# The low part of a weight block: a subtraction on GpSimd, or ScalarE's negative and an adding DMA

## The chip, the core and the metric

The kernel runs on one core of a Trainium2 chip. The metric is device time in microseconds (us) of one execution. The core has a matrix engine (TensorE, rows PE and, for its weight loads, PEld), VectorE (DVE), ScalarE (ACT), GpSimd (POOL) and a queue engine (SP). Each engine works through its own instructions in the order written and waits on semaphores for the others. Copies between memories are done by 16 DMA engines; an instruction on SP, ACT or POOL issues such a copy.

## The reference, cut to what matters

The reference is a two-layer trunk over 1024 tokens of width 1024. What bears on the change is the feed-forward block with a gated unit that ends each layer (width 2816), run twice:

```python
def conv_ffn(h, w_up, conv_w, conv_b, w_down):
    a = dwconv3(h @ w_up, conv_w, conv_b)
    g, u = jnp.split(a, 2, axis=-1)
    return (jax.nn.silu(g) * u) @ w_down
```

The output projection of layer 0's mixer and layer 1's spatial-gating mixer also hold products `h @ W` that are made in the same way.

## The kernel before, in words

**Precision.** TensorE multiplies numbers of a shortened float type (`F32R`, fp32r in the rows). To keep the accuracy of full floats, every operand x is split in two: the high part is x rounded to fp32r, the low part is x minus the high part. A product is then three matmuls into one accumulator, high by high, high by low and low by high (`mm3`). The split is made by `hilo` (line 1149): ScalarE writes the high part into the first half of a new buffer (`A.copy`, line 1152), and VectorE or GpSimd subtracts it from x into the second half (the helper at line 128 issues every plain subtraction, addition and product). The engine that subtracts is chosen by strings of V and G near the top of the file.

**Products.** From the output projection of layer 0 on, every product with a weight takes seven products of half-sized blocks, M1 to M7, in the order M1, M2, M6, M7, M4, M5, M3 (a Strassen scheme). M1 and M2 use blocks of W as they are loaded. Before M6, `wsums` (line 1280) forms S3, S2, S1 and S4 on VectorE, and writes S3, S1 and S4 over the blocks they come from: S3 over the block that M1's split read, S4 over the one that M2's split read. A sum can so start only once the split of that block has read it.

**Up phases** (`up_steps`, line 1289). An up phase of a feed-forward block goes through 22 pairs of 128-wide column tiles of `w_up`; a pair is 7 steps, one per product, of 12 matmuls each, 84 in all. `prep` splits the step's block of W. `use` does the matmuls and then adds the result into the pair's tiles on VectorE (ScalarE for M1). After M3 the pair goes to `post`: for the two tiles a convolution over time (one ScalarE operation, line 1520, and two VectorE operations, line 124, each), Silu on ScalarE (line 1532), a product of the two tiles on VectorE, and, for every second pair, `spill` (line 1410): sums on GpSimd and stores to DRAM that ScalarE issues.

**Down phases** (`down_steps`, line 1344) work through k for each product; a step is again 12 matmuls. Here the other operand is split as well, on GpSimd where it comes from the spilled blocks.

**Who subtracts.** `E_W` gives for each up phase one letter per product M1 to M7, `E_D` for each down phase one letter for k modulo 4:

```python
E_W, E_D = ("VGGVGGG", "VGGVGGG", "GGGVGGG"), ("GVGV", "VVGV", "GVGV", "GVGV", "GVGV")
```

So GpSimd makes 5 of 7 low parts of W in a pair of the first feed-forward block and 6 of 7 in the second one, where M1 is among them.

**Order.** `run` (line 1180) walks through the steps: loads run 8 or 9 steps ahead in the up phases, `prep` 3 steps ahead with a raised priority, and pieces of earlier pairs' convolutions are put in between (`Later`). A scheduler turns this into one fixed order per engine; buffers (`unit`, 40 of 512 KB) are reused as they come free.

Of the kernel before, what the change touches and what calls it, by code (L numbers as in the profile page):

```python
# [20 lines left out]
P = 128  # L21
# [15 lines left out]
# for each phase: how many steps its loads run ahead, and what is made of them, for each product  # L37
# [16 lines left out]
# which of VectorE and GpSimd takes a piece of work: a string for each of the norms, of the phases  # L54
# [15 lines left out]
# Packed per-feature vectors: name, number of 128-row columns.  # L70
# [18 lines left out]
def tile_kernel(ctx: ExitStack, tc: tile.TileContext, ap: dict, out: bass.AP, stop=None):  # L89
# [32 lines left out]
    # ------------------------------------------------------------------ helpers  # L122
# [33 lines left out]
    def eager(main, side):  # L156
        """Emit side as early as its inputs allow (it yields True while they don't)."""
        live = True
        while live:
            for blocked in side:  # L160
                if blocked:
                    break
            else:
                side = iter(())
            try:
                next(main)
            except StopIteration:
                live = False
        for _ in side:
            pass  # L170
# [20 lines left out]
    def mtile(ps, w, hhi, hlo, n=S):  # L191
        """ps [P, n] = W[:, m-tile]^T h, from the unit w of [P, (k, 128)]."""
# [6 lines left out]
    # modulation vectors: 48 columns a layer, and 16 for the context's first norm  # L199
# [25 lines left out]
    def rstd_bcast(acc, n, scale, tp, newps, dg):  # L225
        """acc [P, n], sums of squares -> PSUM [P, n], rstd in every row. dg: [P, n] of scratch."""
# [12 lines left out]
    def bcast(R, r, nt, dg):  # L239
        """R [P, nt*128]: in every row the values of r [P, nt], one column after the other."""  # L240
# [7 lines left out]
    # ================================================================ layer 0  # L248
# [4 lines left out]
    # the blocks of C a product belongs to: (i, l), or (i,) for both l  # L253
# [3 lines left out]
    Hd = dram.tile([2, 2, 2, P, 2048], F32, name="Hd")          # order, half, parity of m  # L257
# [3 lines left out]
    Qd = dram.tile([HEADS, 2, P, S], F32, name="Qd")            # head, hi | lo  # L261
# [9 lines left out]
    def gated_sum(x, gate):  # L271
        """accum for x += gate * C"""
# [10 lines left out]
    def layer0_front(fp):  # L283
        with ExitStack() as es:
# [27 lines left out]
            # ---- filter's network; x^T, context, first modulation columns (shift and scale), norms  # L312
# [4 lines left out]
            def filter_mlp():  # L317
                """sin(f (x w + b)) twice, both halves of time side by side; -> h2s: hi above lo."""
# [10 lines left out]
                def layer(l, rhs, w):  # L329
# [5 lines left out]
                    # u: the angle in turns; less its nearest integer  # L335
# [82 lines left out]
            # ---- DFT over 8 residues of time: frequencies (k + 1/2) pi/1024 + m pi/4, k < 128.  # L418
            # Complex values are R - iS; parts of a tile [P, R|S, 4, CH].
# [6 lines left out]
            def dft(z, n):  # L426
                """z [P s, 8 r, CH] -> X for m = 0, 2, 4, 6 and for m = 1, 7, 5, 3."""
# [37 lines left out]
            def dft_part(z, w, n):  # L465
                """R (w = 0) or S (w = 1) alone -> [P, (m even | m odd), 4, CH]."""
# [14 lines left out]
                add(e(), t[:, 0, 0:2], a[:, w, 0:2], a[:, w, 2:4])      # c0 c1  # L481
                sub(e(), t[:, 0, 2], a[:, w, 0], a[:, w, 2])            # d0
                sub(e(), t[:, 0, 3], a[:, x, 1], a[:, x, 3])            # d1, the other part
# [5 lines left out]
                pm(e(), t[:, 1, 0], b[:, w, 0], b[:, x, 2])             # e0  # L489
                mp(e(), t[:, 1, 1], b[:, w, 0], b[:, x, 2])             # e1  # L490
                u = a
                sub(e(), u[:, 0, 0], b[:, w, 1], b[:, w, 3])            # p
                add(e(), u[:, 0, 1], b[:, x, 1], b[:, x, 3])            # q, the other part
                pm(e(), u[:, 1, 0], u[:, 0, 0], u[:, 0, 1])             # u
                mp(e(), u[:, 1, 1], u[:, 0, 0], u[:, 0, 1])             # v
# [4 lines left out]
            def filters():  # L500
                h2r = h2s.rearrange("p (s r) -> p r s", r=8)
                for o in range(2):
# [14 lines left out]
                    for half in range(2):  # L517
# [4 lines left out]
                        for sd in range(2):  # L522
# [8 lines left out]
                            if sd == 0:  # L531
                                # time 0 has the forward tap alone, (s + d) / 2, and the skip
# [15 lines left out]
            # ---- Hyena's chain: spectrum, product, inverse, gate  # L548
            zs, done = {}, set()

            def spectrum(X, o, half, n):
                """Y = X H, in place."""
# [14 lines left out]
            def idft(Y, n):  # L567
                """Y (m = 0, 2, 4, 6; m = 1, 7, 5, 3) -> Q for r < 4 and for r >= 4."""
# [3 lines left out]
                add(e(), t[:, :, 0:2], ye[:, :, 0:2], ye[:, :, 2:4])   # f0 g0  # L572
                sub(e(), t[:, :, 2:4], ye[:, :, 0:2], ye[:, :, 2:4])   # f1 g1
# [9 lines left out]
                add(e(), u[:, :, 0:2], yo[:, :, 0:2], yo[:, :, 2:4])   # f0 g0  # L583
                sub(e(), u[:, :, 2:4], yo[:, :, 0:2], yo[:, :, 2:4])   # f1 -g1
                O = yo
                add(e(), O[:, :, 0], u[:, :, 0], u[:, :, 1])           # D0
                sub(e(), O[:, :, 2], u[:, :, 0], u[:, :, 1])           # D2
                d = f8()
                sub(e(), d[:, 0, 0], u[:, 0, 2], u[:, 1, 3])           # D1
                add(e(), d[:, 1, 0], u[:, 1, 2], u[:, 0, 3])  # L590
                add(e(), d[:, 0, 1], u[:, 0, 2], u[:, 1, 3])           # D3
                sub(e(), d[:, 1, 1], u[:, 1, 2], u[:, 0, 3])
                add(e(), O[:, 0, 1], d[:, 0, 0], d[:, 1, 0])           # sqrt(2) O1
                sub(e(), O[:, 1, 1], d[:, 1, 0], d[:, 0, 0])
                sub(e(), O[:, 0, 3], d[:, 1, 1], d[:, 0, 1])           # sqrt(2) O3
# [52 lines left out]
            # lambda = exp(q1.k1) - exp(q2.k2) + lambda_init, negated, in every row  # L648
# [11 lines left out]
            # ---- the input projection  # L660
# [11 lines left out]
            def to_time(a):  # L672
                """[P ch, t] -> PSUM [P s, 8 r, P ch], t = 8 s + r."""
# [119 lines left out]
    def attention(fp, x):  # L793
        """x: gets the stream's tiles, to which the first two products of the output projection are added."""
        with ExitStack() as es:
# [39 lines left out]
            def load_head(h):  # L835
                """K: (hi, hi) and (lo, lo), Q: (hi, lo), one above the other, for either map; V."""
# [18 lines left out]
            # A tile of 128 queries goes through: scores and their softmax's sums (m = 0, 1); the maps' difference,  # L855
            # a tile later; its transposes, LAG tiles later; and four tiles together through the values.
# [14 lines left out]
            def factors(q):  # L871
                """p0 - lambda l0/l1 p1, still to be divided by l0"""
# [25 lines left out]
            def values(q):  # L898
                """Six pieces, three a tile, for the two tiles that q ends."""
# [8 lines left out]
            def headnorm(g):  # L908
                """The head's norm, and its way out, in pieces."""
# [17 lines left out]
            # M1, M2 and M6 of the output projection, and what they need  # L927
            wb, spare, aux = {}, [], None

            def two_rows(src, k, n=2):  # L930
                """Tiles k and k + 1 of src's rows."""
# [13 lines left out]
            def operand(name, src):  # L945
                """Loads four tiles of rows; then their parts, one a piece."""
# [11 lines left out]
            def operand3(name, a, b, c, op, tag, last=None):  # L958
                """Of a + b - c (op: add) or a - b + c, likewise; last: tile 3 of a where it isn't in DRAM."""
# [26 lines left out]
            def product(m):  # L986
                """Four pieces of 12 matmuls."""
# [139 lines left out]
    # ================================================================ the rest  # L1127
    # Products W^T h take seven products of half-sized blocks (Strassen's scheme in Winograd's form):
# [31 lines left out]
    class Later:  # L1160
# [3 lines left out]
        @classmethod  # L1164
        def add(cls, gen, wait=0):
            cls.gens.append([gen, wait])
# [258 lines left out]
    def in_place(s, m, k, y, z, t3, first="M6"):  # L1425
# [9 lines left out]
        elif m == "M4":  # L1435
            sub(E(E_J[s], k), z[:, H0], z[:, H0], y[:, H0])    # T4
# [353 lines left out]
```

## Time and profile before

| | |
|---|---|
| median of 3 runs | 2897.93 us (2897.4 to 2901.98) |
| the profiled execution, first to last instruction | 2897.8 us |
| PE busy | 2461.0 us, 85% |
| DVE busy | 2345.8 us, 81% |
| ACT busy | 1075.4 us, 37% |
| POOL busy | 1624.7 us, 56% |
| moved by DMA | 363.93 MB |

The span of the profiled execution and the median of the runs agree to 0.2 us, so nothing that matters lies around the span. Busy time is the time in which an engine had an instruction at work; PE's matmuls overlap, so the mean duration of one is longer than its share of the busy time. An idle time in a row is put down to what ended it: "idle 21.8 <-POOL u L128" is time in which the engine waited for a GpSimd instruction of line 128 that wrote a buffer u.

### The profile page before, as it was taken

To read this page: it belongs to the slowest core of one execution; us is meant where nothing else is said; L and a number is where in the kernel's file an instruction comes from. 1 tells how busy PE (TensorE), PEld (TensorE's weight loads), DVE (VectorE), ACT (ScalarE), POOL (GpSimd) and SP (SyncE) were. 2 spreads that over 40 slices of the span, in tenths; PEclk is the share of its full clock that TensorE was granted. 3 is DMA by queue.
4 is the path that set the end of the run, shared out by engine and by line. 5 is a ranking of instruction groups with operands and counts; after the bars stand their busy time and mean duration, and the time that the engine had idled before them with its cause. 6 is when DMAs were issued, how large, how long until landed. Compare 5 with 4: busy or idle time off the path is not lost. (4 is left out here: it accounts for less than half of the span.)

```text
span 2897.8 us, 29893 instructions
## 1 busy us (share of the span) xinstructions
PE 2461.0 (85%) x10776; PEld 1949.6 (67%) x10776; DVE 2345.8 (81%) x2467; ACT 1075.4 (37%) x1561; POOL 1624.7 (56%) x986
## 2 busy tenths in 40 slices
PE   6899667777988679999998799899669999999897
PEld 2897556565766457777776687677547777776676
DVE  4666887866998889999998987859988888887944
ACT  2322011015764344433343344532254343344242
POOL 1323565545444755645556787535665655657785
PEclk9899878888999889999999999999889999999999
DMA  7243121256732412434347654153021323227322
GB/s 269 69 143 114 66 87 46 84 183 200 209 122 84 174 65 78 161 122 149 118 145 255 231 164 129 44 186 110 23 79 59 100 85 102 86 85 269 133 91 102
DMA packets 137572, 363.93 MB, mean 126 GB/s; under 512 B 12587, under 2 KB 25391, under 8 KB 135248
## 3 DMA queue, kind: packets, MB, share of 16 engines
q1 hardware_dynamic: 90768, 259.25, 27.8%
q10 hardware_dynamic: 46656, 102.78, 9.4%
q8 instruction: 85, 1.39, 0.2%
q14 instruction: 63, 0.52, 0.1%
HBM read 271.80 MB, written 90.18 MB: 125 GB/s over the span
## 5 line engine op out<-in xcount | busy, mean ns | idle before, releaser
L149 PE MATMUL b<-u,u 128*128 128x512 f32 x5780 | 1422.9, 404 | 199.0 <-POOL u L128 125.7
L149 PEld LDWEIGHTS b<-u,u 128*128 128x128 f32 x5780 | 1104.1, 195 | 504.7 <-POOL u L128 172.0
L128 POOL TENSOR_TENSOR u<-u,u 128x512 fp32r<-128x512 f32 (+2 forms) x641 | 1043.3, 1650 | 602.5 <-ACT u L1152 431.2
L128 DVE TENSOR_TENSOR u<-u,u 128x512 f32<-128x512 f32 (+2 forms) x569 | 641.1, 1156 | 169.9 <-ACT u L1152 91.4
L1152 ACT CAST u<-u 128x512 fp32r<-128x512 f32 x772 | 439.1, 616 | 584.9 <-DVE u L128 400.4
L124 DVE SCALAR_TENSOR_TENSOR u<-u,cols,u 128x1023 f32<-128x1023 f32 x176 | 301.2, 1714 | 11.2 <-ACT u L1520 9.9
L128 DVE TENSOR_TENSOR u<-u,b 128x512 f32<-128x512 f32 (+1 forms) x368 | 248.1, 690 | 19.1 <-PE b L149 12.8
L128 POOL TENSOR_TENSOR f<-f 128x256 f32<-128x256 f32 (+2 forms) x99 | 124.7, 1273 | 211.0 <-DVE f L128 183.1
L149 PE MATMUL b<-x,u 128*128 128x512 f32 x1008 | 242.9, 394 | 0.0
L149 PEld LDWEIGHTS b<-x,u 128*128 128x128 f32 x1008 | 188.6, 187 | 46.0
L128 DVE TENSOR_TENSOR f<-f 128x256 f32<-128x256 f32 (+3 forms) x178 | 178.6, 1052 | 1.1
L124 DVE SCALAR_TENSOR_TENSOR x<-b,mods,x 128x512 f32<-128x512 f32 (+1 forms) x140 | 125.0, 938 | 37.2 <-PE b L149 37.2
L149 PE MATMUL pj<-hh,whi 128*128 128x512 f32 x320 | 130.2, 407 | 24.7 <-DVE t L124 14.0
L1520 ACT ACTIVATE u<-u,cols 128x1024 f32<-128x1024 f32 x88 | 109.2, 1244 | 111.3 <-DVE u L128 97.3
L128 POOL TENSOR_TENSOR p<-p,p 128x1280 f32<-128x1280 f32 x27 | 79.5, 2945 | 97.0 <-ACT p L880 76.5
L149 PE MATMUL pj<-hh,wlo 128*128 128x512 f32 x320 | 127.6, 399 | 3.5 <-DVE wlo L128 1.9
L149 PE MATMUL pj<-hl,whi 128*128 128x512 f32 x320 | 128.9, 403 | 0.0
L1532 ACT ACTIVATE u<-u 128x1024 f32<-128x1024 f32 x44 | 46.7, 1061 | 211.3 <-DVE u L124 211.2
L128 POOL TENSOR_TENSOR wlo<-wraw,whi 128x1024 fp32r<-128x1024 f32 x24 | 63.7, 2655 | 76.9 <-ACT whi L143 73.8
L869 ACT ACTIVATE p<-s,nx 128x1280 f32<-128x1280 f32 x64 | 85.0, 1329 | 43.2 <-DVE nx L865 39.2
L149 PE MATMUL s<-f,f 128*128 128x512 f32 (+1 forms) x288 | 82.3, 416 | 17.5 <-ACT t L768 9.9
L865 DVE TENSOR_REDUCE nx<-s 128x1 f32<-128x1280 f32 x64 | 94.5, 1480 | 2.2 <-PE s L149 1.5
(215 smaller groups left out, 2984.7 us busy)
## 6 DMA issues: line engine op xcount, KB each, us to landing
u<-wup SPq DMA_DIRECT2D x88, 512.0 KB, 3.7
Td<-u ACTq DMA_DIRECT2D x66, 512.0 KB, 3.2
u<-Td SPq DMA_DIRECT2D x56, 512.0 KB, 4.4
wraw<-modw SPq DMA_DIRECT2D x48, 512.0 KB, 3.7
u<-wdown SPq DMA_DIRECT2D x40, 512.0 KB, 7.1
wraw<-modw0b SPq DMA_DIRECT2D x32, 512.0 KB, 4.7
xs<-x ACTq DMA_DIRECT2D x48, 256.0 KB, 2.2
x<-xs SPq DMA_DIRECT2D x24, 512.0 KB, 4.1
```

Of the source, the lines that this page charges most:

```text
L124: eng.scalar_tensor_tensor(out=o, in0=a, scalar=sc, in1=b, op0=op0, op1=op1)
L128: eng.tensor_tensor(out=o, in0=a, in1=b, op=op)
L149: T.matmul(o, l, r, start=st, stop=sp)
L865: V.reduce_max(out=q.nx, in_=q.s, axis=AX.X, negate=True)
L869: A.activation(q.p[m], q.s, AF.Exp, bias=q.nx, accum_out=q.l[:, m : m + 1])
L1152: A.copy(out=t[:, H0], in_=x)
L1520: A.activation(a, c, AF.Identity, bias=col(f"fb{l}", f), scale=col(f"fw{l}1", f))
L1532: A.activation(g, g, AF.Silu)
```

## The change

A new function `hilo_w` takes the place of `hilo` at the two places where a block of W is split. Where the string gives VectorE, nothing is changed. Where it gives GpSimd, ScalarE writes the high part as before, then writes minus the high part into the low half, and GpSimd issues a DMA that reads the block of W and adds it to what the low half holds, in SBUF. The change is:

```diff
+    def hilo_w(x, e):
+        if e is V:
+            return hilo(x, e)
+        t = unit(F32R)
+        A.copy(out=t[:, H0], in_=x)
+        A.activation(t[:, H1], t[:, H0].bitcast(F32), AF.Copy, scale=-1.0)
+        G.dma_start(out=t[:, H1], in_=x, accum_op=ADD)
+        return t[:, H0], t[:, H1]
...
-            st_[m] = hilo(q.pop(m), E(E_W[s], int(m[1]) - 1))
+            st_[m] = hilo_w(q.pop(m), E(E_W[s], int(m[1]) - 1))
...
-            bs[m, k] = (hilo(src, E(E_D[s], k % 4)), None if resident else bprep(m, k, bs[m, k]))
+            bs[m, k] = (hilo_w(src, E(E_D[s], k % 4)), None if resident else bprep(m, k, bs[m, k]))
```

The rest of the diff takes comments out of the file.

## Rows read from the trace of the kernel before

**Rows 1.** The page's first part: engine, busy us, share of the span, instructions.
```profile
PE 2461.0 (85%) x10776; PEld 1949.6 (67%) x10776; DVE 2345.8 (81%) x2467; ACT 1075.4 (37%) x1561; POOL 1624.7 (56%) x986
```

**Rows 2.** Stretches: first up phase, second up phase, end of the last down phase.
```profile
core 0: us, PE busy (x) PEld busy (x) DVE busy (x) ACT busy (x) POOL busy (x), PEclk, DMA share, GB/s
1159.00:1521.00 362.00, 335.98 (x1431) 267.22 (x1431) 346.56 (x325) 140.52 (x189) 196.97 (x114) 0.97 0.42 139
2260.00:2608.00 348.00, 323.35 (x1346) 252.69 (x1345) 293.18 (x272) 131.63 (x176) 203.69 (x129) 0.99 0.28 91
...
2750.00:2888.00 138.00, 128.58 (x558) 104.13 (x556) 64.29 (x71) 53.34 (x96) 102.64 (x75) 0.98 0.28 92
```

**Rows 3.** Groups by line and form, second up phase, 2260 to 2608 us.
```profile
line engine op names shapes xcount | busy us, mean ns | idle before us <-releasers
L149 PE MATMUL b<-u,u 128*128 128x512 f32 x1010 | 248.1, 400 | 24.7 <-POOL u L128 21.8 <-ACT u L1152 2.8
...
L128 POOL TENSOR_TENSOR u<-u,u 128x512 fp32r<-128x512 f32 x97 | 159.7, 1660 | 115.1 <-ACT u L1152 115.1
L124 DVE SCALAR_TENSOR_TENSOR u<-u,cols,u 128x1023 f32<-128x1023 f32 x65 | 117.8, 1812 | 7.2 <-ACT u L1520 6.9
...
L128 DVE TENSOR_TENSOR u<-u,u 128x512 f32<-128x512 f32 x48 | 66.1, 1377 | 35.9 <-POOL u L128 35.4
L1152 ACT CAST u<-u 128x512 fp32r<-128x512 f32 x112 | 65.7, 614 | 101.5 <-DVE u L128 101.5
...
L128 POOL TENSOR_TENSOR u<-u,u 128x512 f32<-128x512 f32 x24 | 37.2, 1551 | 29.2 <-DVE u L128 28.6
L128 DVE TENSOR_TENSOR u<-u 128x512 f32<-128x512 f32 x16 | 19.7, 1231 | 0.0
...
L128 POOL TENSOR_TENSOR u<-u 128x512 f32<-128x512 f32 x8 | 10.3, 1288 | 0.0
```

**Rows 4.** The buffers u, same stretch: duration ns, least, median, most; first and last start.
```profile
L124 DVE SCALAR_TENSOR_TENSOR u<-u,cols,u x65: 1283/1716/2318, 2259.3 to 2606.6; 128x1023 f32<-128x1023 f32 x65
...
L128 DVE TENSOR_TENSOR u<-u x16: 683/1230/1782, 2272.9 to 2598.5; 128x512 f32<-128x512 f32 x16
```

**Rows 5.** Groups by line and form, first up phase, 1159 to 1521 us.
```profile
L149 PE MATMUL b<-u,u 128*128 128x512 f32 x1031 | 254.4, 403 | 26.0 <-POOL u L128 19.9 <-DVE u L128 4.4 <-ACT u L1152 1.5
...
L128 POOL TENSOR_TENSOR u<-u,u 128x512 fp32r<-128x512 f32 x82 | 145.8, 1786 | 120.3 <-ACT u L1152 106.0 <-DVE u L128 7.2 <-DVE u L124 4.6
L124 DVE SCALAR_TENSOR_TENSOR u<-u,cols,u 128x1023 f32<-128x1023 f32 x66 | 112.8, 1709 | 1.5 <-ACT u L1520 0.7
...
L128 DVE TENSOR_TENSOR u<-u,u 128x512 f32<-128x512 f32 x49 | 56.8, 1159 | 6.0 <-POOL u L128 5.3
L124 DVE SCALAR_TENSOR_TENSOR u<-wraw,siluc,u 128x1024 f32<-128x1024 f32 x28 | 48.7, 1739 | 0.0
...
L128 DVE TENSOR_TENSOR u<-u,u 128x512 fp32r<-128x512 f32 x32 | 32.3, 1009 | 1.0 <-ACT u L1152 1.0
```

**Rows 6.** Timeline, two pairs of the second up phase: start us, us, instruction [idle before].
```profile
2422.12 2.49 DVE L128 TENSOR_TENSOR u<-u,u 128x512 f32<-128x512 f32 x2 [1.84 <-POOL u L128]
...
2443.45 3.46 DVE L128 TENSOR_TENSOR u<-u,u 128x512 f32<-128x512 f32 x2 [2.48 <-POOL u L128]
...
2420.10 1.14 ACT L1152 CAST u<-u 128x512 fp32r<-128x512 f32 x2 [1.67 <-DVE u L128]
...
2439.61 0.37 ACTq L1414 DMA_DIRECT2D Td<-u  x1
2440.02 1.14 ACT L1152 CAST u<-u 128x512 fp32r<-128x512 f32 x2 [1.70 <-DVE u L128]
...
2440.91 1.29 POOL L128 TENSOR_TENSOR u<-u 128x512 f32<-128x512 f32 x1
```

**Rows 7.** DMA: a queue's packets, MB, share; issues, KB each, median us to landing.
```profile
q1 hardware_dynamic: 90768, 259.25, 27.8%
...
xs<-x ACTq DMA_DIRECT2D x48, 256.0 KB, 2.2
...
q<-Qd SPq DMA_DIRECT2D x8, 256.0 KB, 5.7
```

## The prediction

> **What bounds the kernel now.** I read the page's first part first: VectorE is busy 81% of the span and GpSimd 56% [rows 1], neither a bound over the whole. Then the stretches by stage, since the change sits in the products with weights. By `E_W` and `E_D` it touches 22 x 5 = 110 low parts in the first up phase, 22 x 6 = 132 in the second, 20 in the gating mixer's up phase, and 8 + 21 + 14 + 14 + 42 = 99 in the down phases: 361 in all. Two thirds lie in the two long up phases, so those decide.
>
> In the first one VectorE is busy 346.6 of 362 us, PE 336.0 [rows 2]; in the second VectorE 293.2 of 348 and PE 323.4. Dividing matmuls by 84 gives 1346 / 84 = 16 pairs in 348 us, 21.75 us a pair; the 82 subtractions of the first at five a pair are 16.4 pairs, 22.1 us each [rows 5]. PE waits 24.7 us in the second stretch, 21.8 of it for GpSimd's low parts [rows 3], and 26.0 in the first [rows 5]: 1.5 and 1.6 us a pair. So PE is the floor, some 1.5 us a pair below today, and the loop that keeps it from the floor is to be found.
>
> The timeline shows it for the second phase [rows 6]: ScalarE casts the next pair's M1 and M2 at 2420.10 and 2440.02; VectorE's sum S3, which overwrites what M1's split reads, starts at 2422.12 and 2443.45, ended from waiting by GpSimd both times. From there VectorE works through sums, convolution and product of older pairs; that product releases the store that ScalarE issues at 2439.61, and behind it in ScalarE's queue stand the next casts. The loop is VectorE's work plus the split's path.
>
> The second thing to see is that VectorE's durations have two levels. The convolution's operation takes at least 1283 ns and at most 2318, the sum in place 683 and 1782 [rows 4]; the means, 1812 and 1231, lie between [rows 3]. I take the excess for contention with GpSimd's subtractions, which read SBUF at the same time.
>
> **What the change removes.** 361 GpSimd subtractions of about 1.65 us are some 600 us of GpSimd's 1624.7 [rows 1, 3]. GpSimd is no bound, so this itself is worth nothing; what it frees on VectorE is. Second phase: 65 x (1812 - 1283) + 48 x (1377 - 683) + 16 x (1231 - 683) ns = 34.4 + 33.3 + 8.8 = 76.5 us, or 4.8 a pair [rows 3, 4]. GpSimd keeps the spill's sums, 37.2 + 10.3 of 207.2 us, 23%, so I take 77% of it: 3.7 us a pair. First phase, same minima: 66 x 426 + 49 x 476 + 28 x 456 + 32 x 326 ns = 74.6 us over 16.4 pairs, 4.5, and 77% of it 3.5 us a pair [rows 4, 5].
>
> **What it adds.** On ScalarE one operation more of a cast's size, 614 ns [rows 3]: 3.1 to 3.7 us a pair, where ScalarE is busy 38 to 39% [rows 2]. It stays below 60%, but each cast behind a negative starts 0.57 us later (two casts in 1.14 us [rows 6]). On GpSimd a DMA issue in the subtraction's place; it waits for the negative, and the spill's sums and the next issue stand behind it. None of those is urgent.
>
> The unknown is L, from GpSimd's start of the issue to the landing. The trace has no DMA from GpSimd and none that adds. Below: an issue like ScalarE's, 0.37 us [rows 6], and the landing of a 256 KB store, 2.2 [rows 7], together 2.6. Above: an issue as long as the subtraction, 1.66 [rows 3], and the slowest 256 KB load, 5.7 [rows 7]: 7.4. The addition must read the destination as well. The loads' queue moved 259.25 MB in 27.8% of the span, 806 us [rows 7], so 256 KB take 0.8 us on the engines. I take an issue of 1.0 (between the two), 2.2 for the landing (a store that starts in SBUF is nearest), 0.8 for the second read, and 0.3 for sharing engines that are 28 to 42% busy [rows 2]: L = 4.3 us.
>
> [...]
>
> **The sum, second up phase.** From cast to S3 the path is 2.0 us in one pair and 3.4 in the next [rows 6], mean 2.7. Afterwards: cast and negative 1.14, a semaphore 0.1, then L; in every second pair GpSimd is held by the spill's sums until 2442.20, 2.2 us after the cast instead of 1.25 [rows 6], mean 0.45. That is 1.7 + L, a cost of L - 1.0 = 3.3 us. Against the 3.7 freed: 0.4 us a pair gained, 22 pairs, 9 us. What is late next is M6: S2 can follow only S3, and its own low part goes the same way, to be read by PE two products after M1's. With VectorE's sums at 0.68 us, S3 and S2 take 1.4, the split 1.2 + 0.1 + 4.3, together 7.0 after M1's low part lands; PE needs it after M1 and M2, some 24 matmuls at 0.24 us or 5.8 us. So up to 1.2 us show there; PE's wait today is already 1.5, so I let this take the place of it and not come on top.
>
> **First up phase.** M1's low part is made by VectorE, so only M2's and the later ones go by DMA. M2's split grows from cast plus 1.79 us [rows 5] to cast, 0.61 and L: by L - 1.1 = 3.2 us, and S4 waits for it, behind which stand the additions from PSUM and the convolution. S2 and S1 lie before S4 (1.4 us), so the gain is between 3.5 - 3.2 = 0.3 and 3.5 - 1.8 = 1.7, the latter cut at PE's 1.6. I take 0.8: 18 us over 22 pairs.
>
> **The rest.** The other 119 low parts: at the end of the last down phase PE is busy 128.6 of 138 us [rows 2], and `prep` runs 3 steps, 36 matmuls or 8.6 us, ahead. That lead covers a split longer by 3.2 us, so I cost it at nothing. If the cover is gone, half a microsecond on each would be 60 us; I allow 15 for the range.
>
> Together 27 us: 2898 - 27 = 2871 us. The profiled execution, 2897.8 us, is the median of the runs to 0.2 us, so no correction is due.
>
> **The rivals.** *A short DMA.* With L at most 3.4 (0.37 + 2.2 + 0.8) the split's path costs no more than 2.4, and both phases come down to PE: (1.5 + 1.6) x 22 = 68 us, 2830. For it: the short landings of stores. Against: the 5.7. [...] Chance 0.17.
>
> *The DMA takes it back.* Each microsecond of L costs 22 us in either phase, 44 together, so the change breaks even at L = 4.3 + 27 / 44 = 4.9. At L = 6.2 it is +33 in the second phase (1.5 x 22) and +24 in the first (1.1 x 22): 2955 us; at 7.4, +60 and +51: 3009. For it: a store of 2.2 us is a plain copy, the issue's 1.0 is a guess, and weight loads come in bursts on the same 16 engines. Then VectorE would stand at S3 and S4 and PE at M1, M2 and M6. Chance 0.40.
>
> *Nothing to see.* L from 4.7 to 5.0: within 0.2% (6 us, about what a measurement of this kernel can tell from no change). Chance 0.10.
>
> The forecast itself, L from 3.4 to 4.7, has 0.33. Faster is 0.33 + 0.17 = 0.50, same 0.10, slower 0.40. For the range I go to a little under the short DMA, 2825, and up to L = 6.2, 2960; what lies outside I put at 2 in 10. The likeliest case's own range is 2840 to 2890.
>
> **What would show it.** Right: VectorE's convolution operations near 1.3 us and its sums near 0.7 in both up phases; GpSimd's busy time down by several hundred us; ScalarE up by 361 x 0.61 = 222 us; L near 4.3, its issue near 1.0; a pair near 21.3 us in either phase. Wrong: PE or VectorE waiting for these DMAs longer than for GpSimd today (over 1.6 us a pair), a GpSimd issue that lasts longer than the subtraction, or durations on VectorE that stay at their means, which would say that the contention is not with these subtractions.

## The result

The changed kernel takes 2933.89 us (median of 4 runs, 2929.8 to 2934.83) against 2897.66 us for the kernel before on the same chip: ratio 1.0114, 95% interval [1.01, 1.0129]. It is 36 us slower. The prediction said 2871 us, faster; the time lies inside its range (2825 to 2960), on the other side of no change.

The profiled execution of the changed kernel spans 2932.0 us. First the page's engines and its new DMA queue, which answer to [rows 1] and [rows 7]:

```profile
PE 2469.2 (84%) x10776; PEld 1969.3 (67%) x10776; DVE 2173.1 (74%) x2467; ACT 1272.7 (43%) x1922; POOL 1310.0 (45%) x986
...
q0 software_dynamic: 51984, 94.66, 18.7%
...
u<-u POOLq DMA_DIRECT2D x361, 256.0 KB, 4.6
```

VectorE lost 173 us of busy time and GpSimd 315, ScalarE gained 197 [rows 1]: the work moved as predicted. The groups of the second up phase (2300 to 2650 us) answer to [rows 3], the buffers below them to [rows 4], and the stretches to [rows 2]:

```profile
L149 PE MATMUL b<-u,u 128*128 128x512 f32 x1001 | 236.9, 393 | 33.9 <-DMA u<-u 33.9
...
L124 DVE SCALAR_TENSOR_TENSOR u<-u,cols,u 128x1023 f32<-128x1023 f32 x64 | 82.0, 1281 | 4.5 <-ACT u L1530 3.6
...
L128 DVE TENSOR_TENSOR u<-u,b 128x512 f32<-128x512 f32 x113 | 75.9, 684 | 65.4 <-PE b L149 64.8
```

The last of these groups, VectorE's additions from PSUM, in the kernel before (2260 to 2608 us):

```profile
L128 DVE TENSOR_TENSOR u<-u,b 128x512 f32<-128x512 f32 x111 | 74.1, 679 | 2.3
```

The buffers and the stretches of the changed kernel:

```profile
L124 DVE SCALAR_TENSOR_TENSOR u<-u,cols,u x64: 1275/1283/1287, 2301.9 to 2633.8; 128x1023 f32<-128x1023 f32 x64
```

```profile
1165.00:1530.00 365.00, 335.91 (x1456) 272.09 (x1455) 300.59 (x336) 187.13 (x270) 125.54 (x115) 0.97 0.77 197
2300.00:2650.00 350.00, 312.32 (x1337) 248.53 (x1335) 221.31 (x270) 180.56 (x270) 123.76 (x128) 1.00 0.70 162
```

The reader is to see three things. VectorE's convolution operation takes 1275 to 1287 ns throughout, where it took up to 2318 [rows 4]: the contention is gone. PE's wait grew from 24.7 us [rows 3] to 33.9, and all of it ends with the new DMA. And VectorE's additions from PSUM now wait 64.8 us for PE, where all idle time before them was 2.3. A pair takes 350 x 84 / 1337 = 21.99 us, against 21.75 before. The pairs alternate: from one pair's first matmul to the next's, most of them late in this phase take about 19.9 and 23.6 us in turn before, 19.2 and 24.8 after.

The timeline of a pair of that phase, PE's lines and GpSimd's issues (answers to [rows 6]):

```profile
2432.34 0.86 POOL L1163 DMA_DIRECT2D u<-u  x1 [7.25 <-ACT u L1162]
2434.29 0.86 POOL L1163 DMA_DIRECT2D u<-u  x1 [1.09 <-ACT u L1162]
2435.68 3.02 PE L149 MATMUL b<-u,u 128*128 128x512 f32 x12 [1.66 <-DMA u<-u]
2437.51 1.75 POOL L1163 DMA_DIRECT2D u<-u  x2 [2.36 <-ACT u L1162]
2440.25 5.99 PE L149 MATMUL b<-u,u 128*128 128x512 f32 x25 [1.55 <-DMA u<-u]
```

PE stands still twice within 5 us, each time for a low part that has not landed: M6's, then M7's. By the order of the matmuls, of the 33.9 us 13.2 are waits at M6, 11.0 at M1 and 9.5 at M7. In the first up phase (1165 to 1530 us) PE waits 29.1 us for the new DMA, 23.2 of it at M2. How long one takes is in the statistics of line 1163, the issue's duration and the landing, least, median and most (the landing counts from the issue, so it is the prediction's L):

```profile
L1163 POOL DMA_DIRECT2D u<-u x361: 837/862/2557, 971.1 to 2896.0; - x181
...
DMA to landing us min/median/max: 3.2/4.6/11.1
```

Where the 36 us lie is read from stretches that begin with each stage's first matmul with a weight and end with the next stage's. Before, in this order: first up phase, first down phase, gating mixer as a whole, second up phase, second down phase; then the same of the changed kernel. (The first number after the bounds is the length.)

```profile
1049.00:1557.00 508.00, 462.15 (x1923) 365.47 (x1922) 482.11 (x471) 203.18 (x280) 270.94 (x160) 0.95 0.38 126
1557.00:1811.00 254.00, 226.61 (x982) 180.78 (x983) 210.93 (x193) 109.82 (x192) 193.90 (x120) 0.97 0.58 193
1811.00:2138.00 327.00, 273.64 (x1159) 213.59 (x1158) 267.61 (x324) 126.81 (x201) 185.83 (x125) 0.93 0.27 95
2138.00:2641.00 503.00, 453.34 (x1862) 353.60 (x1860) 428.94 (x418) 201.19 (x278) 294.67 (x183) 0.97 0.27 88
2641.00:2880.00 239.00, 222.18 (x935) 177.69 (x933) 150.65 (x141) 93.28 (x166) 189.43 (x131) 0.97 0.43 149
```

```profile
1049.00:1562.00 513.00, 458.37 (x1921) 367.01 (x1921) 411.84 (x476) 270.59 (x396) 180.20 (x163) 0.94 0.71 181
1562.00:1824.00 262.00, 235.75 (x984) 189.43 (x983) 208.78 (x186) 117.33 (x208) 161.78 (x116) 0.93 0.67 208
1824.00:2163.00 339.00, 279.43 (x1164) 218.80 (x1162) 260.39 (x328) 155.53 (x254) 154.04 (x128) 0.91 0.49 129
2163.00:2676.00 513.00, 447.63 (x1860) 354.97 (x1859) 337.17 (x417) 270.81 (x408) 184.54 (x183) 0.96 0.66 154
2676.00:2913.00 237.00, 219.84 (x933) 177.58 (x932) 151.22 (x139) 112.95 (x204) 148.63 (x127) 0.97 0.68 193
```

The up phases lost 5 and 10 us where 18 and 9 were to be gained. Of the stages costed at nothing, the first down phase lost 8 us and the gating mixer 12; the second down phase is 2 us shorter than before. In the gating mixer what grew is PE's wait for VectorE, here before and after, and its wait for the DMA (16.1 us after):

```profile
PE b L149 <- DVE u L128: 7.9, 6, 2.9
PE b L149 <- DVE u L128: 18.7, 7, 4.5
```

### The profile page after: what moved, and what is told of

Read it like the earlier page. It is cut to its first block, busy times and chain, and to the rows that moved or that the text cites. A ratio compares the mean times of both kernels' runs of the same rounds, so it can differ in the third digit from the quotient of the medians.

```text
span 2932.0 us, 30865 instructions
## 1 busy us (share of the span) xinstructions
PE 2469.2 (84%) x10776; PEld 1969.3 (67%) x10776; DVE 2173.1 (74%) x2467; ACT 1272.7 (43%) x1922; POOL 1310.0 (45%) x986
## 3 DMA queue, kind: packets, MB, share of 16 engines
q1 hardware_dynamic: 90768, 259.25, 27.4%
q0 software_dynamic: 51984, 94.66, 18.7%
## 5 line engine op out<-in xcount | busy, mean ns | idle before, releaser
L149 PEld LDWEIGHTS b<-u,u 128*128 128x128 f32 x5780 | 1117.0, 197 | 529.0 <-DMA u<-u 192.2
L128 DVE TENSOR_TENSOR u<-u,u 128x512 f32<-128x512 f32 (+2 forms) x569 | 568.1, 1027 | 226.9 <-ACT u L1152 110.6
L1163 POOL DMA_DIRECT2D u<-u x361 | 327.5, 950 | 649.6 <-ACT u L1162 534.6
L128 POOL TENSOR_TENSOR u<-u,u 128x512 fp32r<-128x512 f32 (+2 forms) x280 | 447.3, 1657 | 251.2 <-ACT u L1152 124.7
L1161 ACT CAST u<-u 128x512 fp32r<-128x512 f32 x361 | 215.8, 614 | 390.8 <-DVE u L128 274.1
L1152 ACT CAST u<-u 128x512 fp32r<-128x512 f32 x411 | 240.7, 614 | 168.7 <-DVE u L128 68.3
L124 DVE SCALAR_TENSOR_TENSOR u<-u,cols,u 128x1023 f32<-128x1023 f32 x176 | 227.1, 1294 | 9.4 <-ACT u L1530 7.5
L1162 ACT ACTIVATE u<-u 128x512 fp32r<-128x512 f32 x361 | 220.4, 626 | 31.4 <-POOL u L128 20.6
L143 ACT CAST whi<-wraw 128x1024 fp32r<-128x1024 f32 x28 | 29.3, 1049 | 161.7 <-PE pj L149 141.6
```

Source lines behind the costliest of these rows:

```text
L124: eng.scalar_tensor_tensor(out=o, in0=a, scalar=sc, in1=b, op0=op0, op1=op1)
L128: eng.tensor_tensor(out=o, in0=a, in1=b, op=op)
L143: A.copy(out=hi, in_=x)
L149: T.matmul(o, l, r, start=st, stop=sp)
L1152: A.copy(out=t[:, H0], in_=x)
L1161: A.copy(out=t[:, H0], in_=x)
```

## The experiments

Ratios are to the kernel before, run on the same chip; an interval is 95%.

### Which stages lose

In `e1_up_only` the new function stands in the up phases alone (262 DMAs), in `e2_down_only` in the other stages alone (99).

```diff
-            bs[m, k] = (hilo_w(src, E(E_D[s], k % 4)), ...     # e1_up_only
+            bs[m, k] = (hilo(src, E(E_D[s], k % 4)), ...
-            st_[m] = hilo_w(q.pop(m), E(E_W[s], int(m[1]) - 1))  # e2_down_only
+            st_[m] = hilo(q.pop(m), E(E_W[s], int(m[1]) - 1))
```

> The change in the up phases alone (262 DMAs); the down phases keep GpSimd's subtraction. By the phases of the two traces the up phases of the feed-forward blocks lost some 12 us and the down phases and the mixer's products the other 22, so under theory A this run is 2905 to 2918 us. Theory B, a loss in proportion to the number of DMAs: 2898 + 36 x 262 / 361 = 2924 us.

> The change in the down phases alone (99 DMAs); the up phases keep GpSimd's subtraction. Theory A: the down phases have no VectorE loop that the freed contention could shorten, so all of the longer split that shows is loss: 2910 to 2922 us. Theory B, in proportion: 2898 + 36 x 99 / 361 = 2908 us. What I predicted (a lead of 8.6 us covers it): 2898 us.

Measured: 2910.27 us, 1.0032 [1.0021, 1.0042], and 2917.89 us, 1.0061 [1.004, 1.0081]. The 99 DMAs cost 18 us, the 262 only 10.

### What the DMA takes, and what waiting for it takes

`e3_no_dma` leaves the DMA out. `e4b_unwaited` issues an adding DMA of the same size at the same place, but into a spare place in DRAM, so that nobody waits for its landing. `e4_unwaited` was a first form of it.

```diff
-        G.dma_start(out=t[:, H1], in_=x, accum_op=ADD)                              # e3_no_dma
+        G.dma_start(out=spare[1][spare[0]], in_=cols[:, 0:512], accum_op=ADD)       # e4_unwaited
+        G.dma_start(out=spare[1][spare[0]], in_=t[:, H1].bitcast(F32), accum_op=ADD)  # e4b_unwaited
```

> As the changed kernel, but GpSimd's adding DMA is left out, so that the low part holds minus the high part (the low part of the weights is not computed); ScalarE's extra operation stays. Theory A, the landing is what costs (4.6 us from issue, waited for by TensorE and by VectorE's sums S3 and S4): without it the freed VectorE time shows, and the kernel comes down to TensorE, 2810 to 2850 us. Theory B, the traffic on the 16 DMA engines is what costs: the same. Theory C, ScalarE's 361 extra operations and the casts pushed back by them are what costs: it stays at 2890 us or above.

> As the changed kernel, but the 361 DMAs add a constant block to a spare tensor in DRAM, 16 places in turn, instead of to the low part (which is then minus the high part, the low part of the weights is not computed): the same number of GpSimd issues and adding DMAs of the same size, and nobody waits for their landing. Theory A (the landing): near the kernel without the DMA, at most 10 us above it. Theory B (the traffic): most of the way back to the changed kernel, 2910 us or more, with loads of w_up and w_down landing as late as there. Issues cost (0.9 us each on GpSimd) would show here too, but GpSimd is at 45%.

> As the changed kernel, but each DMA takes ScalarE's negative from the low part and adds it to a spare tensor in DRAM (16 places in turn): it is issued at the point where the changed kernel issues its own, moves as much, and TensorE and the sums do not wait for its landing (the low part stays minus the high part, so the low part of the weights is not computed). In the run before this one the DMAs hung on nothing and were issued during layer 0's first part, so they did not meet the feed-forward blocks. Theory A (the landing): 2727 to 2760 us, near the kernel without the DMA. Theory B (the traffic): 2880 us or more.

Measured: `e3_no_dma` 2726.54 us, 0.9399 [0.9385, 0.9413]; `e4b_unwaited` 2790.51 us, 0.9624 [0.9596, 0.9651]. `e4_unwaited` (2891.1 us, 0.9967 [0.9952, 0.9983]) tells little: its DMAs depend on nothing, so they were issued during layer 0, which they slowed. `e3_no_dma` is 84 us below the lowest time expected, and `e4b_unwaited` lies between its two theories: part of the DMA's cost is there without any wait for a landing. The up phases of `e4b_unwaited`:

```profile
1049.00:1497.00 448.00, 439.83 (x1921) 358.27 (x1922) 412.95 (x476) 269.32 (x396) 180.98 (x162) 0.98 0.84 203
...
2094.00:2537.00 443.00, 431.01 (x1860) 350.38 (x1859) 352.50 (x417) 275.43 (x411) 194.41 (x184) 0.99 0.83 178
```

They are as short as with no DMA (451 and 443 us in `e3_no_dma`), though the DMA engines are busier than in the changed kernel. So in the up phases the whole cost is the wait for the landing: 513 - 448 = 65 and 513 - 443 = 70 us; the freed contention is worth 508 - 448 = 60 and 503 - 443 = 60. In the second one every pair but the first three, which are interleaved, now takes 19.2 us. In the first down phase and the gating mixer, however, `e4b_unwaited` takes 268 and 329 us, far above `e3_no_dma` (239 and 313) and near the changed kernel (262 and 339), with nobody waiting.

### Can the wait be taken off in the up phases

`e5_late_dma` uses the DMA in the up phases only for M7, M5 and M3, the late products. `e7_own_sums` gives S3 and S4 a buffer of their own, so that VectorE's sums need not wait for the split. `e9_early_v` gives M1, M2, M4 and M6 to VectorE, M3, M5 and M7 to the DMA, and leaves the down phases as before. `e10_before_v` has the same letters and no DMA, `e11_before_vv` VectorE for all seven, both in the kernel before.

```diff
+            st_[m] = (hilo_w if m in ("M7", "M5", "M3") else hilo)(q.pop(m), ...)       # e5_late_dma
+        s2, n = unit()[:, H0], unit()                                                # e7_own_sums
+        sub(E(e, 0), n[:, H0], a11, a21)
...
+        sub(E(e, 3), n[:, H1], a12, s2)
+E_W = "VVGVGVG", "VVGVGVG", "VVGVGVG"       # e9_early_v, e10_before_v
+E_W = "VVVVVVV", "VVVVVVV", "VVVVVVV"       # e11_before_vv
```

> In the up phases only M7, M5 and M3 get their low part by DMA; M2, M6 and, in the second feed-forward block, M1 keep GpSimd's subtraction; the down phases as changed. Theory A: the low parts that are needed soonest, M1 and M6, are no longer late by a landing, so the up phases come below those of the kernel before; with the down phases' loss of some 20 us the whole is 2880 to 2905 us. If only the contention freed counts, half of it is given back: 2915 to 2930 us.

> As the changed kernel, but S3 and S4 are written to a buffer of their own, so they no longer wait until the DMAs of M1 and M2 have read the blocks. If the chain through S3 is the loss, as my prediction's sum had it: 2870 to 2900 us. If TensorE's own wait for the low parts of M1 and M6 is: 2915 to 2935 us. More buffers in use could make it slower than the changed kernel.

> In the up phases VectorE, which the change freed, makes the low parts of M1, M2, M4 and M6, and DMAs those of M3, M5 and M7, which are needed last; the down phases keep GpSimd's subtraction. Theory A: no landing is needed early, GpSimd keeps only the spill's sums: 2820 to 2870 us, faster than both kernels. Theory B (the traffic, now 144 DMAs): 2895 us or more.

> The kernel before, with the letters of e9_early_v (VectorE makes the low parts of M1, M2, M4 and M6, GpSimd those of M3, M5 and M7) and no DMA. If the gain of e9_early_v (2839.6 us) comes from the letters alone, this one lies at 2835 to 2850 us as well. If the three DMAs that are left on late products carry their part of it, by taking GpSimd's subtractions away from beside VectorE, the kernel keeps VectorE's convolution operations at 1.5 us or more and lies near 2870 us (about half the gain).

> The kernel before, with VectorE making all seven low parts of W in the up phases; no DMA and no subtraction of W on GpSimd there. If what GpSimd's subtractions cost VectorE is as large as what they take off it, this is no slower than before: 4 to 5 more subtractions of 0.7 us a pair, 3 to 3.5 us, against 3.7 us of contention freed, 2880 to 2905 us. If VectorE's own time sets the up phases, it is slower: up to +1.0 us in each of 44 pairs, 2940 us.

Measured: `e5_late_dma` 2895.3 us, 0.9984 [0.9969, 0.9998]; `e7_own_sums` 2915.51, 1.0055 [1.0038, 1.0072]; `e9_early_v` 2839.64, 0.98 [0.9771, 0.9828]; `e10_before_v` 2855.49, 0.9844 [0.9827, 0.9862]; `e11_before_vv` 2824.59, 0.9737 [0.9722, 0.9751].

With the late products alone on the DMA the up phases last 507 and 480 us. A buffer for the sums gives back 18 us of the 36. The second up phase falls from 513 to 492 us, but there PE still waits 39.2 us for the DMA, of 56.9 in the changed kernel, now at M1 and M2 and hardly at M6: the landing is needed by PE itself and not only by the sums. The letters bring most of the gain of `e9_early_v`; its DMAs add at most 16 us, 10 of them in the second up phase. In the first up phase `e9_early_v` is slower than `e10_before_v`, 502 us against 497. And the DMA is not needed at all: `e11_before_vv`, expected at 2880 us or above, is faster than all of these. Its second up phase:

```profile
2113.00:2563.00 450.00, 435.97 (x1857) 351.29 (x1857) 433.87 (x547) 198.00 (x276) 85.55 (x50) 0.98 0.30 98
```

VectorE has 129 more operations there than before (547 against 418) and is busy 5 us longer (433.87 against 428.94). What GpSimd's subtractions took from VectorE through contention was about as much as the subtractions themselves cost VectorE, and the split no longer crosses to GpSimd.

### What the 99 DMAs cost in the other stages

`e12_down_none` is `e2_down_only` without its DMAs, `e13_down_small` has them with 16 of 512 columns.

```diff
-        G.dma_start(out=t[:, H1], in_=x, accum_op=ADD)                      # e12_down_none
+        G.dma_start(out=t[:, 512:528], in_=x[:, 0:16], accum_op=ADD)         # e13_down_small
```

> The changed function in the down phases and the gating mixer's output projection alone, with its DMA left out (the low parts of those 99 blocks are only the negative of the high part, not the low part). The sum of what the same stages gained in e3_no_dma, 14 + 6 + 27 us, says 2850 to 2860 us. If the stages' cost came from ScalarE's second operation and not from the DMA, it lies near 2900 us or above.

> As e2_down_only (2917.9 us), with each of its 99 DMAs adding the first 16 of 512 columns only (the other columns of the low part are left as the negative of the high part). The same number of issues on GpSimd, waits and semaphores, a 32nd of the bytes. If the loss in these stages is the bytes on the 16 DMA engines beside the loads of weights and blocks, it is gone: near e12_down_none, 2850 to 2870 us. If it is the issue on GpSimd and the wait for it, it stays: 2905 to 2920 us. About half way if landing time is the cause, since a small transfer still takes some 3 us to land.

Measured: 2851.21 us, 0.983 [0.9806, 0.9855], and 2909.29 us, 1.003 [1.0009, 1.0052]. Of 67 us between `e12_down_none` and `e2_down_only`, the bytes make 9 at most, for the intervals of `e2_down_only` and `e13_down_small` overlap; 58 are there with a 32nd of the bytes. So the bytes are not the main cost. On the landing this pair says less, since a DMA of 16 columns still takes 2.8 us to land in `e13_down_small` (median; 4.6 for 256 KB in the changed kernel). `e4b_unwaited` says more. The first down phase, the gating mixer and the second down phase together take 769 us in `e3_no_dma`, 828 in `e4b_unwaited`, where the issues are back and no landing is waited for, and 838 in the changed kernel. So the landing is not the main cost of these stages either. An issue and its wait are no longer than the subtraction that they replace (1042 and 562 ns in `e13_down_small`, 1660 before [rows 3]), and GpSimd is not what PE comes to wait for: in these three stages PE waits 17.4 us for GpSimd's line 128 in `e4b_unwaited`, 16.0 in `e3_no_dma`, but 41.5 us for VectorE's, against 12.0.

What differs is found among VectorE's operations. These are durations by buffers in the changed kernel (least, median, most):

```profile
L128 DVE TENSOR_TENSOR u<-u,u x569: 673/687/10266, 968.8 to 2899.0; 128x512 f32<-128x512 f32 x94, 128x512 fp32r<-128x512 f32 x87, 128x1024 f32<-128x1024 f32 x9
L128 DVE TENSOR_TENSOR u<-u,b x368: 670/681/1220, 1075.0 to 2678.3; 128x512 f32<-128x512 f32 x178, 128x1024 f32<-128x1024 f32 x6
...
L124 DVE SCALAR_TENSOR_TENSOR u<-wraw,siluc,u x49: 1272/1279/8851, 1177.0 to 1742.7; 128x1024 f32<-128x1024 f32 x49
...
L128 DVE TENSOR_TENSOR u<-x,u x30: 676/686/9634, 1036.7 to 2210.4; 128x512 fp32r<-128x512 f32 x30
```

Single operations with two operands in SBUF last up to 10.3 us; in the kernel before none of these three groups exceeds 2.9. Those with an operand in PSUM (b) stay below 1.3. A stretch of the timeline, VectorE and GpSimd, shows how it comes about:

```profile
1577.49 0.88 POOL L1163 DMA_DIRECT2D u<-u  x1
1577.55 0.69 DVE L128 TENSOR_TENSOR u<-u,u 128x512 fp32r<-128x512 f32 x1 [1.15 <-ACT u L1152]
1578.11 4.07 POOL L128 TENSOR_TENSOR u<-u,u 128x512 f32<-128x512 f32 x3
1578.16 8.85 DVE L124 SCALAR_TENSOR_TENSOR u<-wraw,siluc,u 128x1024 f32<-128x1024 f32 x1
1581.85 1.57 POOL L128 TENSOR_TENSOR u<-u 128x512 f32<-128x512 f32 x1
1583.11 2.81 POOL L128 TENSOR_TENSOR u<-u,u 128x512 fp32r<-128x512 f32 x2
```

GpSimd issues a DMA at 1577.49 and goes on without a pause through six subtractions, until 1585.92. VectorE's operation begins at 1578.16 and ends at 1587.01, 1.1 us after the last of them: about its own length of 1.27. It had no turn while the run lasted. All 18 operations of two SBUF operands over 3 us that the trace shows from 960 us on began in such a run behind an issue, and together they last 95 us longer than their plain 0.68 or 1.28 us each. They lie in the down phases, the gating mixer and the projections, where GpSimd still splits the activation's blocks; in the up phases, where few subtractions are left to GpSimd, there is one of 3.4 us.

Two pairs of kernels test it. `e18_g_copy` is the kernel before, subtraction included, where GpSimd in addition issues a copy of 16 columns to DRAM that nobody reads, after each of the 99; in `e19_sp_copy` SP issues the same copies, on its own queue. `e15_dma_blocks_v` is `e2_down_only` with the activation's blocks split on VectorE in the two feed-forward down phases, so that nothing stands behind the issues there; `e14_blocks_v` is its control, the kernel before with those blocks on VectorE.

```diff
+        h, l = hilo(x, e)                                                   # e18, e19
+        if e is not V:
+            G.dma_start(out=spare[1][spare[0]], in_=l[:, 0:16].bitcast(F32))   # e19: nc.sync
-        return bload, lambda m, k, b: hilo(b)                                # e14, e15
+        return bload, lambda m, k, b: hilo(b, V)
```

> The kernel before, and after each of the 99 GpSimd low parts of W in the down phases and the gating mixer's output projection GpSimd issues a plain copy of 16 columns of it to a spare place in DRAM, which nobody reads or waits for. If an issue before a run of subtractions shuts VectorE out, VectorE shows some 10 to 20 operations of 3 to 10 us where the kernel before has none over 2.9, and the time is 2920 to 2970 us. If it is only the issue's 1 us on GpSimd, no operation on VectorE exceeds 3 us; the kernel is then slower only by what GpSimd's 99 us more cost, 0 to 60 us.

> The same 99 copies, issued by SP. Both theories expect no VectorE operation over 3 us and a time within 0.5% of the kernel before; a loss here would be the copies themselves, or loads that stand behind them in SP's queue.

> The kernel before, with the low parts of the activation's blocks in the feed-forward down phases made by VectorE in place of GpSimd; no DMA. It is the control of e15_dma_blocks_v. About 260 subtractions change sides; both theories expect it between 2860 and 2910 us, with no VectorE operation above 3 us in the down phases.

> e2_down_only (the DMA in the down phases and the gating mixer's output projection) with the same blocks on VectorE, so that no run of GpSimd subtractions stands behind the issues in the feed-forward down phases. If shutting VectorE out is the cause, no VectorE operation there lasts over 3 us, and the kernel is no slower than e14_blocks_v in those two phases (within 0.3% over all, or faster by up to 1%; the gating mixer's projection, whose blocks stay on GpSimd, may keep 7 us of loss). If the issue's time, the landing or the bytes are the cause, it is slower than e14_blocks_v by the 15 to 20 us that e2_down_only lost.

Measured: `e18_g_copy` 2965.63 us, 1.0212 [1.0186, 1.0238]; `e19_sp_copy` 2906.45, 1.0011 [0.9998, 1.0025]; `e14_blocks_v` 2896.75, 0.9973 [0.9959, 0.9986]; `e15_dma_blocks_v` 2890.83, 0.9961 [0.9939, 0.9984].

The same copies cost 64 us when GpSimd issues them and 4 when SP does, an amount whose interval holds no change. From 960 us on, 20 operations of VectorE last over 3 us in `e18_g_copy` (up to 12.4), none in `e19_sp_copy` (up to 2.9). GpSimd's own busy time is 1632.7 us, 8 more than before: its 56 us of issues are made up by shorter subtractions, so GpSimd's time cannot be the 64 us. What PE waits for says the same. These are its waits for line 128 of GpSimd and of VectorE, in `e18_g_copy` and then in `e19_sp_copy` (us, times, longest):

```profile
PE b L149 <- POOL u L128: 119.6, 87, 9.9
PE b L149 <- DVE u L128: 80.3, 29, 10.3
```

```profile
PE b L149 <- POOL u L128: 121.5, 99, 5.2
PE b L149 <- DVE u L128: 32.7, 20, 6.2
```

Of the 59 us between the two kernels, 48 are PE's waits for VectorE. First `e18_g_copy`, VectorE's buffers; then a stretch of its timeline:

```profile
L128 DVE TENSOR_TENSOR u<-u,u x569: 671/737/12369, 967.8 to 2928.5; 128x512 f32<-128x512 f32 x93, 128x512 fp32r<-128x512 f32 x85, 128x1024 f32<-128x1024 f32 x12
```

```profile
1598.91 0.56 POOL L1161 DMA_DIRECT2D spare<-u  x1
1599.49 4.97 POOL L128 TENSOR_TENSOR u<-u,u 128x512 fp32r<-128x512 f32 x4
...
1600.97 12.84 DVE L128 TENSOR_TENSOR u<-u,u 128x512 fp32r<-128x512 f32 x2
1604.41 0.56 POOL L1161 DMA_DIRECT2D spare<-u  x1
1604.99 6.14 POOL L128 TENSOR_TENSOR u<-u,u 128x512 fp32r<-128x512 f32 x5
...
1612.18 1.22 PE L149 MATMUL b<-u,u 128*128 128x512 f32 x2 [10.28 <-DVE u L128]
```

and the same group of buffers in `e19_sp_copy`:

```profile
L128 DVE TENSOR_TENSOR u<-u,u x569: 674/955/2879, 962.5 to 2860.9; 128x512 f32<-128x512 f32 x92, 128x512 fp32r<-128x512 f32 x86, 128x1024 f32<-128x1024 f32 x12
```

A low part that VectorE should have made waits 11.2 us, through eight of these nine subtractions and the issue among them, and PE waits 10.28 us for it: the price of one shut-out on the path. With the runs of subtractions taken away the DMA does no harm. In `e15_dma_blocks_v` the longest such operation of the first down phase takes 2.5 us, and the two down phases last 245 and 228 us, against 251 and 232 in the control. The gating mixer, whose blocks stay on GpSimd, keeps operations of up to 7.5 us and a loss: 340 us against 329. GpSimd has little else to do in the two down phases of either kernel, so this pair alone does not tell the shut-outs from GpSimd's time; the copies do.

### The best version

`e16_all_v` has no DMA, and VectorE makes every low part of W. `e17_dma_rest_v` is `e15_dma_blocks_v` with VectorE for the up phases.

```diff
+E_W, E_D = ("VVVVVVV",) * 3, ("VVVV",) * 5      # e16_all_v, in the kernel before
+E_W = ("VVVVVVV",) * 3                           # e17_dma_rest_v, in e15_dma_blocks_v
```

> The kernel before with VectorE making every low part of W from the output projection on; no DMA. e11_before_vv (up phases alone) measured 2824.6 us. If a subtraction less on GpSimd is worth its cost on VectorE in the down phases as it was in the up phases, 2800 to 2820 us; if VectorE is full there, 2825 to 2850 us.

> VectorE makes all low parts of the up phases, the changed function is left in the down phases and the gating mixer's output projection, and the activation's blocks of the feed-forward down phases are split with VectorE. If the DMA pays where nothing of GpSimd's stands behind its issue, this adds what e15_dma_blocks_v has over the kernel before to e11_before_vv: 2810 to 2822 us. If it does not, it is at or above e11_before_vv's 2824.6 us.

Measured: 2797.08 us, 0.9651 [0.9636, 0.9665], and 2810.81 us, 0.9701 [0.9676, 0.9727]. `e16_all_v` is 101 us faster than the kernel before and, by the two ratios, some 135 faster than the changed one. Its page's first part:

```profile
PE 2433.4 (87%) x10776; PEld 1943.1 (70%) x10776; DVE 2395.0 (86%) x2828; ACT 1073.9 (38%) x1561; POOL 1059.1 (38%) x625
```

VectorE took over 361 operations and is busy 49 us longer [rows 1].

## Why the prediction was wrong

**What bounds the kernel, and what the change frees: the mechanism right, the sizes not.** VectorE's long operations were contention with GpSimd's subtractions; in the second up phase the median of the convolution's operation fell from 1716 ns [rows 4] to 1283, its least before. Nor was the 23% kept back for the spill's sums needed: in the second up phase no such operation exceeds 1287 ns. With the landing out of the way (`e4b_unwaited`) that is worth 60 us in either up phase, where PE as the floor was to allow 68 us in both. The floor was set too high: it took off PE's waits of 1.5 and 1.6 us a pair, but PE's busy time fell too, from 462 to 440 and from 453 to 431 us, the mean granted clock being 0.98 and 0.99 in place of 0.95 and 0.97.

**L: a little short.** Predicted 4.3 us; measured 4.6 in the second up phase and 5.0 in the first, the issue 0.86 of it in place of 1.0, so the landing was what was short. The semaphore ahead of it, 0.1 in the sum and in no row, took 0.29 (median of the second up phase, from the end of ScalarE's negative to the issue). The least of the 361 is 3.2 and the median 4.6, where the rival of the short DMA needed 3.4 at most, so it falls. From their share of 18.7% of 16 engines' span, the new queue's packets took an estimated 1.5 us for each of the 361, where a load's 256 KB took 0.8 [rows 7], which fits the second read that the sum allowed for. At 4.6 and 5.0 the prediction's own sum still gives 0.1 us a pair gained in either phase, which is its rival "Nothing to see"; measured, the pair of the second became 0.24 us longer.

**The step that failed in the up phases** is the sum's balance of 3.3 us of longer path against 3.7 us freed, with M6's lateness to "take the place of" PE's wait "and not come on top". Of the 3.7 us only 2.55 can show in the second up phase, from a pair of 21.75 to PE's 19.2; the landing takes 2.8 of it back, to 22.0. So the cost was below the forecast, and what it was set against further below. PE's wait did not stay either: it is 33.9 / (1337 / 84) = 2.13 us a pair against 24.7 / 16 = 1.54, an addition of 0.59. M6 has 0.83 of it, within the 1.2 forecast; the rest is at M1 and M7, and in the first up phase most is at M2, where the sum had priced the landing only by way of S3 and S4 and not as a wait of PE's own. While PE waits for landings, VectorE waits for PE, and its work no longer sets the pair. The path through S3 still counts: a buffer of their own for the sums (`e7_own_sums`) gives back 21 us of the second up phase. `e4b_unwaited` shows the landing as the whole cost: 65 and 70 us over the phases, with their first and last pairs 3.0 and 3.2 us a pair.

**The other step that failed** is "the rest", 119 low parts costed at nothing because `prep` runs 8.6 us ahead. That this covers them was read from one stretch, the end of the last down phase, and there it held: the second down phase is no longer than before. It did not hold in the first down phase, 8 us longer, and in the gating mixer, 12 us longer, where PE was busy only 274 of 327 us before. The lead was set against a split longer by 3.2 us. It was no lead against VectorE being shut out for up to 10 us by GpSimd, a mechanism that the trace of before could not show, since no DMA was issued from GpSimd there. The 99 DMAs alone lose 18 us, half of the 36 (`e2_down_only`), where without the DMA the same stages gain 51 (`e12_down_none`). Of the 67 us between, at most 9 are the bytes; that an issue can shut VectorE out and what this can cost is shown by `e18_g_copy` against `e19_sp_copy`, and that the loss in the feed-forward down phases goes when GpSimd's runs of subtractions go by `e15_dma_blocks_v` against `e14_blocks_v`. The allowance of 15 us was near the size, for another reason.

**The rivals.** "The DMA takes it back" was the nearest: PE and VectorE did come to stand for the landing. But its price was to come from L above 4.9 in the up phases; L was 4.6 and 5.0, and these phases lost 15 of the 36 us.

**What stays open.** Why GpSimd keeps VectorE out for a whole run behind an issue (8.85 us at 1578.16 in the changed kernel), where in the kernel before, without one, both go on, was not found. It does not do so every time: some of the long operations ended before the run did, and from 985 us on in `e18_g_copy` five subtractions behind an issue alternate with operations of VectorE of 1.6 to 1.8 us. How the other 58 us divide between the shut-outs, the landing and the 0.95 us (mean) that each issue holds GpSimd was not measured in the changed kernel itself, nor is it settled that the second down phase loses nothing: with the DMA in these stages alone (`e2_down_only`) it took 246 us. In the first down phase PE's waits are no longer than before in all, 26.2 us after and 27.4 before. The 8 us lost there are busy time, up by 9 us with the same matmuls, at a mean granted clock of 0.93 after and 0.97 before: more of the time at the lower of the levels (0.50 of full speed, not 1.00, in stretches of 2 us). Single waits of more than 3 us rose from one to five, and each of the seven falls of the clock stands beside a wait of PE's of 1.9 to 3.7 us. No run varied the clock by itself.

## What to carry to other kernels

Where two engines slow each other, price a piece of work by what it takes from both: in the second up phase 129 operations more on VectorE cost it only 5 us (`e11_before_vv`), because the contention had cost about as much. A DMA in the place of an operation pays only where its landing, 4.6 us for 256 KB within SBUF, has slack, and an issue on GpSimd with a run of its own arithmetic behind it is to be avoided (99 of them cost 64 us in `e18_g_copy`, against 4 from SP): take the arithmetic away or, for a plain copy, issue from SP (an adding DMA from another engine was not tried). A cover read from one stage holds for that stage. Cost a stage at nothing only against every engine that its lead must cover, and not only the one that was changed.

## What the runs showed of the hardware

Behind a DMA issue on GpSimd that GpSimd operations on SBUF follow without a pause, a VectorE operation of two SBUF operands could last as long as the run: 8.85 us through six subtractions in the changed kernel, 11.2 through eight in `e18_g_copy`, where the longest took 12.4. In the kernel before, where GpSimd issues no DMA, both engines go on: beside 17 subtractions that GpSimd made without a pause in 26 us (from 1589.88) VectorE made 19 operations, the longest of 2.3 us, and from 960 us on none of VectorE's operations lasts more than 2.9. Those with an operand in PSUM were not held: from 960 us on none takes more than 1.29 us before, in the changed kernel or in `e18_g_copy`, and in the changed kernel four of them, from 1718.75 on, took 1.27 us each while GpSimd went through three subtractions behind an issue.

In the changed kernel an issue of 128 rows takes GpSimd 0.84 us at least, 0.86 in the median and 2.56 at most when adding 256 KB. With 16 columns the median is no less (0.88 us in `e13_down_small`; the mean of the 99 is 1.04, and 1.02 with 256 KB in `e2_down_only`), and a plain copy of 16 columns takes 0.56 in `e18_g_copy`. Between the adding DMAs it does not go with the bytes.
